# Tile offsets of 512 bytes, a feed-forward entered by 128 tokens first, and the order of matvec products

## Chip, core and metric

One core of a Trainium2 chip runs the whole program. The metric is the device time of one execution in microseconds, as the median of several runs. Numbers of the trace come from one further execution under the hardware profiler.

## What is computed

Two layers of a decoder trunk for 256 tokens of width 2048, all in float32. Every sub-layer adds `gate * f(RMSNorm(x) * (1 + scale) + shift)` to `x`, and the six vectors of a layer come from a conditioning vector `c` by one large matvec:

```python
cond = jax.nn.silu(c)
for l in range(DEPTH):
    mod = cond @ ada_w[l] + ada_b[l]
    sh1, sc1, g1, sh2, sc2, g2 = jnp.split(mod, N_MOD, axis=-1)
    h = modulate(rmsnorm(x, norm_mix_g[l]), sh1, sc1)
    y = mixer_ab(h, ...) if l % 2 == 0 else mixer_c(h, ...)
    x = x + g1[:, None, :] * y
    h = modulate(rmsnorm(x, norm_ffn_g[l]), sh2, sc2)
    x = x + g2[:, None, :] * swiglu(h, ffn_w1[l], ffn_w3[l], ffn_w2[l])
return rmsnorm(x, final_g)
```

`swiglu` is `(silu(h @ w1) * (h @ w3)) @ w2` with 5632 hidden columns. `mixer_ab` (layer 0) has an input projection to 4096 columns, a causal convolution over 31 tokens on one half, a gated mixing within chunks of 128 tokens on the other, and an output projection; `mixer_c` (layer 1) pools over 2 to 16 tokens.

## The kernel before

**Products.** A float32 product is made of three products of a shorter type: both operands are split into a high part (`hi` of a weight, `ah`, `mh` or `hh` of an activation) and the rest (`lo`; `al`, `ml`, `hl`), and hi x high, hi x rest and lo x high are added up in one PSUM bank (lines 255, 256 and 261). The tokens are the stationary side: 128 columns of an activation tile are loaded as weights, and 512 columns of a weight tile stream by. Weights are loaded by SyncE as `raw` tiles of 512 KB (two blocks of 128 rows by 512 columns, 12 buffers), and `split` (L206, L207) makes `hi` on ScalarE and `lo` on VectorE, with 4 buffers each. A `unit` does 512 rows of one weight for both halves of the tokens (b = 0 and 1): 24 products. A `block` splits two units ahead and runs all their products for b = 0, then all for b = 1, and calls hooks on the way. Activations of the mixers and of the first feed-forward product stand in `ah`/`al` (`mh`/`ml` share these places), the hidden ones, which the second product `w2` reads, in `hh`/`hl`, in a pool that is opened after all the others.

**Where tiles lie.** Pools lie one behind the other in each partition, and each tile is rounded up to 32 bytes. As built, the activation tiles begin at byte 36,384 of a partition, `raw` at 69,152, `hi` at 118,304 and `lo` at 134,688, and all their sizes are multiples of 512: each of them begins 32 bytes past a multiple of 512. The work pool's tiles begin at 171,552. The pool of the hidden tiles `hh`/`hl` begins at 195,936, which is 352 past a multiple of 512, and all of its tiles have this offset.

**Matvecs.** The `ada_w` products run in the background, in steps between units (`tick`, with a rate of steps per unit in RATES). Some vectors are made on TensorE: `mod` (L354) and `mod_cols` (L420) load two raw tiles a step and issue four matmuls of 32 rows, j = 0, 1 from the tile loaded first and j = 2, 3 from the one loaded last, into four strips of one bank. Others are summed up on VectorE (`weighed`, L390 and L392), with a column sum (`ps_col`, L448) at the end. `shift[0]` and `shift[1]` are the two halves of the vector that shifts the first feed-forward's input.

**The seam into the first feed-forward.** The mixer's output projection ends in `tail`: a block whose b = 0 products come first, so that the residual (L707, L708), the squares (L507) and the norm (`rstd`: L514, L516, and `r` on GpSimd, L518) of the first 128 tokens start while b = 1 runs. `ffn` then calls `e.prep` for the other quarters and for b = 1: `xr` (here on ScalarE, since `lean` is set, L527), four transposes (L532), a copy `xT` (L570). `started` closes the generators of the first quarter's scale and shift, makes `h`, `ah` and `al` (L552 or L554, L541, L542) for both halves, and runs three units for each quarter q of the 2048 input columns; the third one's banks are `mt`. Between units it advances the generators of the next quarters. Instructions of one engine run in the order in which a scheduler put them at build time, with semaphores between engines.

Of the kernel before, what the change touches and what calls it, by code (L numbers as in the profile page):

```python
# [8 lines left out]
F32 = mybir.dt.float32  # L9
F32R = mybir.dt.float32r  # L10
AF = mybir.ActivationFunctionType
ALU = mybir.AluOpType
PSUM = bass.MemoryType.PSUM
ENG = mybir.EngineType
# [3 lines left out]
P = 128  # L18
# [9 lines left out]
PADC = 16  # L28
EPS = 1e-6
RAW, HL = 12, 4  # L30
RATES = 1.28, 0.71, 0.5, 1.0, 1.0
PE2 = False
PE3 = True
FILL = 5
# [6 lines left out]
class Trunk:  # L41
# [6 lines left out]
    def __init__(self, ctx, tc, ins, out):  # L48
        self.ctx, self.tc, self.nc = ctx, tc, tc.nc
        self.i, self.out = ins, out  # L50
        self.bg = []
        self.credit = 0.0
        self.late = []
        self.fill = []
        self.lean = False

        def pool(name, bufs, **kw):
            return ctx.enter_context(tc.tile_pool(name=name, bufs=bufs, **kw))

        self.cpool = pool("const", 1)  # L60
        self.xpool = pool("resid", 1)
        self.apool = pool("act", 1)
        self.rawp = pool("raw", RAW)
        self.hip = pool("whi", HL)
        self.lop = pool("wlo", HL)
        self.accp = pool("acc", 1)
        self.gp = pool("gate", 2)
        self.wk = pool("work", 2)
        self.mmp = pool("mmp", 4, space=PSUM)
        self.tpp = pool("tpp", 2, space=PSUM)  # L70
        self.adap = pool("adap", 1, space=PSUM)
        self.msp = pool("msp", 1, space=PSUM)


    def consts(self):
        nc, c = self.nc, self.cpool
        i = self.i
        warm = c.tile([P, 1], F32, name="warm")
        nc.vector.memset(warm, 0.0)
        nc.scalar.activation(warm, warm, AF.Silu)  # L80
        self.ident = c.tile([P, P], F32, name="ident")
        make_identity(nc, self.ident)
        self.identr = c.tile([P, P], F32R, name="identr")
        nc.vector.tensor_copy(self.identr, self.ident)
        self.ones = c.tile([P, P], F32, name="ones")
        nc.vector.memset(self.ones, 1.0)
        self.mhalf = c.tile([P, 1], F32, name="mhalf")
        nc.gpsimd.memset(self.mhalf, -0.5)
        self.pick = c.tile([P, 1], F32, name="pick")
        nc.gpsimd.memset(self.pick, 0.0)  # L90
        for j in range(4):
            nc.gpsimd.memset(self.pick[32 * j : 32 * j + 1, :], 1.0)
# [251 lines left out]
    def mod(self, l, v, on_pe, then):  # L344


        nc = self.nc
        w = self.i["ada_w"][l]
        if on_pe:
            ps = self.adap.tile([P, 512], F32, name="ps_ada", tag="ada")  # L350
            for k in range(KT):
                raws = [self.load_wide(w, k * P, v * D + DH * h)[0] for h in range(2)]
                for j in range(4):
                    nc.tensor.matmul(  # L354
                        ps[32 * j : 32 * j + 32, :], self.cond[:, k : k + 1].to_broadcast([P, 32]),
                        raws[j // 2][:, j % 2, :], start=k == 0, stop=k == KT - 1, skip_group_check=True,
                    )
                if k < KT - 1:
                    yield
        else:  # L360
            ps = None
            for hh in range(2):
                acc = self.accp.tile([P, DH], F32, name="acc", tag="acc")
                for _ in self.weighed(acc, l, v * D + DH * hh):
                    yield
                if ps is None:
                    ps = self.adap.tile([P, 512], F32, name="ps_ada", tag="ada")
                for j in range(2):
                    o = 32 * (2 * hh + j)
                    nc.tensor.matmul(  # L370
                        ps[o : o + 32, :], self.ones[:, :32], acc[:, 512 * j : 512 * j + 512],
                        start=True, stop=True, skip_group_check=True,
                    )
                if hh == 0:
                    yield
        rows = self.wk.tile([P, 512], F32, name="rows", tag="rows", bufs=1)
        nc.vector.tensor_tensor(
            rows, ps, self.load_rows(self.i["ada_b"][l, v * D : (v + 1) * D]), op=ALU.add
        )
        then(rows)  # L380
        yield
# [25 lines left out]
    def mod_cols(self, l, v, q, on_pe, dst, gname=None, staged=False):  # L407
# [6 lines left out]
            acc = self.accp.tile([P, 512], F32, name="accq", tag="acc")  # L414
        for u in range(4):
            raws = [self.load(self.i["ada_w"][l], 512 * u + 256 * h, v * D + 512 * q) for h in range(2)]
            for j in range(4):
                k = 4 * u + j
                if on_pe:
                    nc.tensor.matmul(  # L420
# [100 lines left out]
    def transposed(self, b, q, r):  # L521
# [1 line left out]
        nc = self.nc  # L523
        xr = self.wk.tile([P, 512], F32, name="xr", tag="t", bufs=3)
        src = self.x[b][:, 512 * q : 512 * q + 512]
        if self.lean:
            nc.scalar.activation(xr, src, AF.Copy, scale=r)  # L527
        else:
            nc.vector.tensor_scalar(xr, src, r, None, op0=ALU.mult)
        ps = self.tpp.tile([P, 4, P], F32, name="tp", tag="tp")  # L530
        for a in range(4):
            nc.tensor.transpose(ps[:, a, :], xr[:, P * a : P * a + P], self.ident)  # L532
# [115 lines left out]
    def started(self, e, w_cols, rate):  # L648

        self.rate = 0.0
        ps = [self.banks(), self.banks()]
        ps.append([self.tpp.tile([P, 512], F32, name=f"mt{b}", tag="tp") for b in range(NB)])
        for g in e.parts[0]:
            self.close(g)
        for q in range(4):
            e.act[q] = [self.scaled(e.act[q][b], q, b, e.gs, e.sh) for b in range(NB)]
            nxt = e.parts[q + 1] if q < 3 else ()
            more = e.parts[2][1:] if q == 0 else ()  # L660
            for u, (w, col0) in enumerate(w_cols):
                self.unit(
                    w, 512 * q, col0, e.act[q], ps[u], q == 0, q == 3, lambda: self.between(nxt, 2 * u, more)
                )
                self.between(nxt, 2 * u + 1, more)
        self.rate = rate
        return ps

# [41 lines left out]
            self.sumsq(b, q)  # L710


    def mixer_ab(self, e, nxt):
        nc, i = self.nc, self.i
        with ExitStack() as s:
            p = s.enter_context(self.tc.tile_pool(name="ab", bufs=1))
# [57 lines left out]
                for _ in extra:  # L774
                    pass
            self.rate = RATES[0]
            self.lean = True
            act = e.act

            co = p.tile([P, HT, T], F32, name="co", tag="co")  # L780
# [138 lines left out]
            def out_half(half):  # L919
                for n in range(4):  # L920
# [5 lines left out]
                        self.residual(ps[b], self.g1, n, b, half == 0)  # L926

                    if half == 0 and n == 3:
                        self.tail(cells, resid, nxt)
                    else:  # L930
                        self.chain(cells)
# [72 lines left out]
    def ffn(self, p, l, e, nxt, gen_g2, rest):  # L1004
# [4 lines left out]
        held = {}  # L1009
        act = e.act  # L1010
        if e.parts:
            for q in range(1, 4):
                e.prep(0, q)
            for q in range(4):
                e.prep(1, q)
            ps = self.started(e, [(w1, 0), (w3, 0), (w1, 512)], RATES[1])
            self.lean = False
            held = {(1, 0): ps[0], (3, 0): ps[1], (1, 1): ps[2]}
        else:
            ps = self.begun(e, [(w1, 0), (w3, 0), (w1, 512)], rest)  # L1020
# [74 lines left out]
    def run(self):  # L1095
# [16 lines left out]
        self.gen_g1 = self.add(self.bcast(0, G1, True, self.g1))  # L1112
        scale = [self.mod_cols(0, SC2, q, True, ffn0.gs, "ffn_g") for q in range(4)]
        shift = [self.mod_full(0, SH2, ffn0.sh, None, (hh,)) for hh in range(2)]
        self.add(*scale, *shift)
        ffn0.parts = [(scale[0], shift[0]), scale[1:2], (scale[2], shift[1]), scale[3:]]
        self.mixer_ab(mix0, ffn0)

        self.g2 = self.gate()
        g2 = self.add(self.bcast(0, G2, False, self.g2))  # L1120
# [77 lines left out]
```

## Time and profile before

| | |
|---|---|
| median of 3 runs | 2008.23 us (2002.36 to 2008.52) |
| the profiled execution | 2001.65 us, of it a span of 1999.9 us |
| mean granted TensorE clock | 0.984 |
| TensorE matmuls busy | 1950.2 us, 8896 records |
| VectorE / ScalarE busy | 1408.9 / 849.8 us |
| HBM | 536.68 MB read, 269 GB/s over the span |

Times in views are microseconds from the span's start unless marked ns. A row of a group reads: line, engine, operation, out<-in, shapes, count, then busy time and the mean ns of one, then idle time of the engine before it and what ended it. A matmul's own duration overlaps the next one's, so the pace is read from starts or from counts in a window. In rows of the timeline the first two numbers are start and duration. In the chain of work the second is what the piece adds to it.

### The profile page before, as it was taken

The page shows a single profiled execution, that of the slowest core. Times are in us where ns is not written, and L with a number is a line of the kernel's source. Part 1 is how long each engine was busy: PE and PEld are TensorE (multiplying, and loading weights), DVE is VectorE, ACT ScalarE, POOL GpSimd, SP SyncE. Part 2 cuts the span into 40 slices and gives each one's busy share as a digit, 9 for nine tenths or more (in the row PEclk, how much of TensorE's full clock was granted, in tenths as well). Part 3 has the DMA queues.
Part 4 walks back from the last instruction along what each step waited for, and adds up shares of the span by engine and source line. Part 5 has one row for each costly group of instructions (what it writes and reads, how often), then busy time and mean ns, then how long its engine had stood idle before and what let it go on. Part 6 is the DMA issues. An engine that isn't in the chain of part 4 may idle for free.

```text
span 1999.9 us, 24247 instructions
## 1 busy us (share of the span) xinstructions
PE 1950.2 (98%) x8896; PEld 1539.9 (77%) x8896; DVE 1408.9 (70%) x1650; ACT 849.8 (42%) x1047; POOL 33.9 (2%) x92
## 2 busy tenths in 40 slices
PE   6899999989999999999999999999999999999998
PEld 3566667768887888887878877888788888888886
DVE  2678999796878878777887788877455445554455
ACT  3244343465444334433344346544434444334443
POOL 0000000000000000000210000000000000000000
PEclk7899999989999999999999999999999999999999
DMA  9998988798989899888988887988556665566551
GB/s 350 366 358 281 339 273 277 277 343 278 322 299 327 314 311 347 313 295 304 327 325 297 281 289 264 332 280 309 194 189 190 190 190 191 178 196 192 189 184 48
DMA packets 246248, 540.39 MB, mean 270 GB/s; under 512 B 16521, under 2 KB 17849, under 8 KB 245744
## 3 DMA queue, kind: packets, MB, share of 16 engines
q1 hardware_dynamic: 245840, 537.79, 77.9%
q8 instruction: 69, 1.13, 0.2%
q10 hardware_dynamic: 288, 1.05, 0.1%
q14 instruction: 51, 0.42, 0.1%
HBM read 536.68 MB, written 2.10 MB: 269 GB/s over the span
## 4 chain that ended last, share of the span: by engine, by line
PE 93%; DMA 3%; DVE 2%; ACT 1%; issue 0%; SPq 0%; POOL 0%; POOLq 0%; DVEq 0%; ACTq 0%
PE mm L255 28%; PE mm L256 27%; PE mm L261 27%; PE ps_ada L420 1%; DMA raw<-in_ab_w_in_dram 1%; PE ps_col L448 1%; PE mt L255 1%; PE tp L699 1%; PE mt L256 1%; PE mt L261 1%; PE ps_ada L354 1%; PE tp L532 1%; DMA x<-in_x_dram 1%; DVE accq L427 1%; DMA raw<-in_ada_w_dram 1%; PE tp L965 1%
## 5 line engine op out<-in xcount | busy, mean ns | idle before, releaser
L206 ACT CAST hi<-raw 128x1024 fp32r<-128x1024 f32 x632 | 663.8, 1052 | 1010.9 <-PE mm L256 902.8
L207 DVE TENSOR_TENSOR lo<-raw,hi 128x1024 fp32r<-128x1024 f32 x632 | 771.0, 1224 | 426.0 <-ACT hi L206 419.2
L255 PE MATMUL mm<-hi,ah 128*128 128x512 f32 x1568 | 618.7, 395 | 4.7 <-ACT hi L206 3.7
L256 PE MATMUL mm<-hi,al 128*128 128x512 f32 x1568 | 613.5, 391 | 0.0
L261 PE MATMUL mm<-lo,ah 128*128 128x512 f32 x1568 | 422.1, 390 | 0.0
L255 PEld LDWEIGHTS mm<-hi,ah 128*128 128x128 f32 x1568 | 295.6, 189 | 89.3 <-ACT hi L206 16.0
L261 PEld LDWEIGHTS mm<-lo,ah 128*128 128x128 f32 x1568 | 295.0, 188 | 61.6
L256 PEld LDWEIGHTS mm<-hi,al 128*128 128x128 f32 x1568 | 296.0, 189 | 60.2
L255 PE MATMUL mm<-hi,hh 128*128 128x512 f32 x704 | 278.9, 396 | 0.0
L256 PE MATMUL mm<-hi,hl 128*128 128x512 f32 x704 | 278.1, 395 | 0.0
L392 DVE SCALAR_TENSOR_TENSOR acc<-raw,cond,acc 128x1024 f32<-128x1024 f32 x210 | 269.1, 1281 | 7.0 <-DMA raw<-in_ada_w_dram 5.1
L261 PE MATMUL mm<-lo,hh 128*128 128x512 f32 x704 | 194.7, 395 | 0.0
L255 PEld LDWEIGHTS mm<-hi,hh 128*128 128x128 f32 x704 | 132.0, 187 | 33.9 <-ACT hi L206 1.7
L261 PEld LDWEIGHTS mm<-lo,hh 128*128 128x128 f32 x704 | 132.0, 187 | 32.2
L256 PEld LDWEIGHTS mm<-hi,hl 128*128 128x128 f32 x704 | 132.1, 188 | 31.8
L803 DVE SCALAR_TENSOR_TENSOR co<-aT,cw,co 128x256 f32<-128x256 f32 x240 | 100.1, 484 | 0.0
L420 PE MATMUL ps_ada<-raw,cond 128*32 128x512 f32 x352 | 60.9, 659 | 6.4 <-DMA raw<-in_ada_w_dram 5.7
L255 PE MATMUL mm<-hi,mh 128*128 128x512 f32 x160 | 65.1, 408 | 1.6 <-ACT mh L541 1.6
L256 PE MATMUL mm<-hi,ml 128*128 128x512 f32 x160 | 64.6, 406 | 0.3 <-DVE ml L542 0.3
L707 DVE TENSOR_TENSOR gy<-mm,gate 128x512 f32<-128x512 f32 x72 | 47.0, 686 | 23.9 <-PE mm L261 23.6
L427 DVE SCALAR_TENSOR_TENSOR accq<-raw,cond,accq 128x512 f32<-128x512 f32 x75 | 56.3, 751 | 9.7 <-DMA raw<-in_ada_w_dram 7.8
L255 PE MATMUL mt<-hi,ah 128*128 128x512 f32 x96 | 40.7, 424 | 7.2 <-ACT hi L206 7.2
(170 smaller groups left out, 993.7 us busy)
## 6 DMA issues: line engine op xcount, KB each, us to landing
raw<-in_ffn_w_dram SPq DMA_DIRECT2D x528, 512.0 KB, 4.8
raw<-in_ada_w_dram SPq DMA_DIRECT2D x384, 512.0 KB, 5.6
raw<-in_ab_w_in_dram SPq DMA_DIRECT2D x64, 512.0 KB, 7.9
raw<-in_ab_w_out_dram SPq DMA_DIRECT2D x32, 512.0 KB, 6.6
raw<-in_pool_w_dram SPq DMA_DIRECT2D x8, 512.0 KB
x<-in_x_dram SPq DMA_DIRECT2D x2, 1024.0 KB
gate<-in_final_g_dram SPq DMA_DIRECT2D x1, 1024.0 KB
out_dram<-x SPq DMA_DIRECT2D x2, 512.0 KB, 3.8
```

What stands on the lines that cost most here:

```text
L206: nc.scalar.copy(hi, raw)
L207: nc.vector.tensor_tensor(lo, raw, hi.bitcast(F32), op=ALU.subtract)
L255: nc.tensor.matmul(ps[b], act[b][0][:, kk, :], hi[:, k, :], start=first and kk == 0, stop=False)
L256: nc.tensor.matmul(ps[b], act[b][1][:, kk, :], hi[:, k, :], start=False, stop=False)
L261: self.nc.tensor.matmul(ps[b], act[b][0][:, kk, :], lo[:, k, :], start=False, stop=last and kk == 3)
L354: nc.tensor.matmul(ps[32 * j : 32 * j + 32, :], self.cond[:, k : k + 1].to_broadcast([P, 32]), raws[j // 2][:, j % 2, :], start=k == 0, st ...
L392: nc.vector.scalar_tensor_tensor(acc, raw, self.cond[:, k : k + 1], acc, op0=ALU.mult, op1=ALU.add)
L420: nc.tensor.matmul(acc[32 * j : 32 * j + 32, :], self.cond[:, k : k + 1].to_broadcast([P, 32]), raws[j // 2][:, j % 2, :], start=u == 0, s ...
L427: nc.vector.scalar_tensor_tensor(acc, raws[j // 2][:, j % 2, :], self.cond[:, k : k + 1], acc, op0=ALU.mult, op1=ALU.add)
L448: nc.tensor.matmul(ps[:, a : a + 1], src[:, P * a : P * a + P], one, start=u == 0, stop=u == len(parts) - 1,)
L707: nc.vector.tensor_tensor(t, ps, g[:, 512 * q : 512 * q + 512], op=ALU.mult)
L803: nc.vector.scalar_tensor_tensor(co[:, k, :], src, cw[:, k, j : j + 1], co[:, k, :], op0=ALU.mult, op1=ALU.add,)
```

## The change

Four things change.

Offsets: two constants of one column each become one tile, and a tile of 192 bytes that nothing uses stands at the head of the work pool. As built, the activation tiles begin at 36,352, `raw` at 69,120, `hi` at 118,272, `lo` at 134,656 and the hidden tiles at 196,096, all of which are multiples of 512. The work pool's other tiles begin 192 past one.

Matvecs on TensorE: the four products of a step go in the order 2, 3, 0, 1. The background's rate in the first mixer is 1.31 in place of 1.28.

Seam: the scale and `shift[0]` generators are finished ahead of the mixer's `tail`; `shift[1]` is added behind the mixer. `started` makes the first quarter's tile for b = 0 alone, runs the first two units as a `block` (24 products for b = 0, then 24 for b = 1) and calls the other `prep`s and the scaling for b = 1 from its hooks. `xr` is always made on VectorE, and `lean` holds inside `started` alone.

```diff
-RATES = 1.28, 0.71, 0.5, 1.0, 1.0
+RATES = 1.31, 0.71, 0.5, 1.0, 1.0
...
         self.wk = pool("work", 2)
+        self.wk.tile([P, 48], F32, name="gap", tag="gap", bufs=1)
...
-        self.mhalf = c.tile([P, 1], F32, name="mhalf")
+        two = c.tile([P, 2], F32, name="two")
+        self.mhalf, self.pick = two[:, :1], two[:, 1:]
         nc.gpsimd.memset(self.mhalf, -0.5)
-        self.pick = c.tile([P, 1], F32, name="pick")
...
                 raws = [self.load_wide(w, k * P, v * D + DH * h)[0] for h in range(2)]
-                for j in range(4):
+                for j in (2, 3, 0, 1):
...
             raws = [self.load(self.i["ada_w"][l], 512 * u + 256 * h, v * D + 512 * q) for h in range(2)]
-            for j in range(4):
+            for j in (2, 3, 0, 1) if on_pe else range(4):
...
-        if self.lean:
-            nc.scalar.activation(xr, src, AF.Copy, scale=r)
-        else:
-            nc.vector.tensor_scalar(xr, src, r, None, op0=ALU.mult)
+        nc.vector.tensor_scalar(xr, src, r, None, op0=ALU.mult)
...
         ps = [self.banks(), self.banks()]
+        act = e.act[0]
+
+        def scale(b):
+            act[b] = self.scaled(act[b], 0, b, e.gs, e.sh)
+
+        self.soon(scale, 0)
+        todo = [(e.prep, 1, 0), (e.prep, 0, 1), (e.prep, 1, 1), (scale, 1), (e.prep, 0, 2), (e.prep, 1, 2), (e.prep, 0, 3)]
+        slots = [(0, 1), (0, 2), (0, 3), (1, 0), (1, 1), (1, 2), (1, 3)]
+        self.block(
+            [(w, 0, col0, act, ps[u], True, False) for u, (w, col0) in enumerate(w_cols[:2])],
+            {at: [lambda c=c: self.soon(*c)] for at, c in zip(slots, todo)},
+        )
+        e.prep(1, 3)
         ps.append([self.tpp.tile([P, 512], F32, name=f"mt{b}", tag="tp") for b in range(NB)])
-        for g in e.parts[0]:
-            self.close(g)
+        self.lean = True
         for q in range(4):
-            e.act[q] = [self.scaled(e.act[q][b], q, b, e.gs, e.sh) for b in range(NB)]
+            if q > 0:
+                e.act[q] = [self.scaled(e.act[q][b], q, b, e.gs, e.sh) for b in range(NB)]
             nxt = e.parts[q + 1] if q < 3 else ()
             more = e.parts[2][1:] if q == 0 else ()
+            if q == 0:
+                last = [n for n in self.nc.cur_bb.bb.instructions if n.engine == ENG.DVE][-1]
+                with self.tc.issue_after(last):
+                    for slot in range(2):
+                        self.between(nxt, slot, more)
             for u, (w, col0) in enumerate(w_cols):
+                if q == 0 and u < 2:
+                    continue
                 self.unit(
-                    w, 512 * q, col0, e.act[q], ps[u], q == 0, q == 3, lambda: self.between(nxt, 2 * u, more)
+                    w, 512 * q, col0, e.act[q], ps[u], q == 0, q == 3,
+                    lambda: (self.between(nxt, 2 * u), self.between((), 0, more)),
                 )
-                self.between(nxt, 2 * u + 1, more)
+                self.between(nxt, 2 * u + 1)
+                for _ in range(2):
+                    self.between((), 0, more)
+        self.lean = False
...
                     if half == 0 and n == 3:
+                        self.finish(scale)
                         self.tail(cells, resid, nxt)
...
-            for q in range(1, 4):
-                e.prep(0, q)
-            for q in range(4):
-                e.prep(1, q)
             ps = self.started(e, [(w1, 0), (w3, 0), (w1, 512)], RATES[1])
-            self.lean = False
...
-        self.add(*scale, *shift)
+        self.add(*scale, shift[0])
+        last_shift = shift[1]
...
-        self.mixer_ab(mix0, ffn0)
+        self.mixer_ab(mix0, ffn0, [*scale, shift[0]])
+        self.add(last_shift)
```

In the order of the built program, TensorE at the seam before: `ps_col` is the column sum of `shift[0]`, `tp` the transposes, `ah_3506`/`al_3507` the first quarter's tile for b = 0.

```order
L448 MATMUL ps_col<-ones,acc 128x1 x8
L532 MATMUL tp<-ident,xr 128x128 x24
L255 MATMUL mm_3495<-hi,ah_3506 128x512
L532 MATMUL tp<-ident,xr 128x128 x4
L256 MATMUL mm_3495<-hi,al_3507 128x512
L532 MATMUL tp<-ident,xr 128x128 x4
```

And now, where `ah_3434`/`al_3435` are that tile:

```order
L262 MATMUL mm_3315<-lo,mh_2917 128x512 x2
L530 MATMUL tp<-ident,xr 128x128 x12
L256 MATMUL mm_3425<-hi,ah_3434 128x512
L257 MATMUL mm_3425<-hi,al_3435 128x512
L530 MATMUL tp<-ident,xr 128x128 x4
L256 MATMUL mm_3425<-hi,ah_3434 128x512
L257 MATMUL mm_3425<-hi,al_3435 128x512
L530 MATMUL tp<-ident,xr 128x128 x4
```

The column sum has gone ahead, into the mixer's tail; 12 transposes in place of 24 stand before the first product (of b = 0 and, among them, of b = 1), and the rest between products.

VectorE at the same place before: `s` and `m` lead to the norm, `gy`/`x` are the residual of the mixer's last columns, `sh` is the shift from the column sum.

```order
L707 TENSOR_TENSOR gy<-mm_3292,gate 128x512
L392 SCALAR_TENSOR_TENSOR acc<-raw,cond,acc 128x1024
L708 TENSOR_TENSOR x_114<-x_114,gy 128x512
L392 SCALAR_TENSOR_TENSOR acc<-raw,cond,acc 128x1024
L207 TENSOR_TENSOR lo<-raw,hi 128x1024
L514 TENSOR_REDUCE s<-ss 128x1
L454 TENSOR_TENSOR sh_119<-ps_col,adab 128x8
L516 TENSOR_SCALAR m<-s 128x1
L390 TENSOR_SCALAR acc<-raw,cond 128x1024
L707 TENSOR_TENSOR gy<-mm_3293,gate 128x512
L392 SCALAR_TENSOR_TENSOR acc<-raw,cond,acc 128x1024
L708 TENSOR_TENSOR x_115<-x_115,gy 128x512
```

And now:

```order
L208 TENSOR_TENSOR lo<-raw,hi 128x1024 x2
L515 TENSOR_REDUCE s<-ss 128x1
L517 TENSOR_SCALAR m<-s 128x1
L527 TENSOR_SCALAR xr<-x_114,r 128x512
L730 TENSOR_TENSOR gy<-mm_3315,gate 128x512
L731 TENSOR_TENSOR x_115<-x_115,gy 128x512
L552 TENSOR_SCALAR h_3429<-xT_3393,gs_118,sh_119 128x128 x2
L515 TENSOR_REDUCE s<-ss 128x1
L517 TENSOR_SCALAR m<-s 128x1
L527 TENSOR_SCALAR xr<-x_115,r 128x512
L527 TENSOR_SCALAR xr<-x_114,r 128x512
L540 TENSOR_TENSOR al_3435<-h_3429,ah_3434 128x512
```

The sums of `shift[1]` (L390, L392; L391, L393 now) no longer stand among these; the first of them comes behind the last `xr`, eight rows further down. Two splits stand before the first half's `s`, and the second half's norm and `xr` before the first half's `al`.

TensorE at the column sum of `shift[1]` before, within the second quarter's second unit (`ah_3656`):

```order
L261 MATMUL mm_3497<-lo,ah_3656 128x512 x2
L261 MATMUL mm_3498<-lo,ah_3665 128x512 x2
L448 MATMUL ps_col<-ones,acc 128x1 x8
L255 MATMUL mm_3497<-hi,ah_3656 128x512
L256 MATMUL mm_3497<-hi,al_3657 128x512
```

And now, where `ah_3810` is the third quarter's first tile, which needs that shift:

```order
L262 MATMUL mt_3582<-lo,ah_3656 128x512 x2
L262 MATMUL mt_3583<-lo,ah_3665 128x512 x2
L449 MATMUL ps_col<-ones,acc 128x1 x8
L256 MATMUL mm_3425<-hi,ah_3810 128x512
L257 MATMUL mm_3425<-hi,al_3811 128x512
```

The sum has moved behind the last product of the second quarter, right before the first of the third.

More of the change, by code (lines that the diff above doesn't have):

```diff
@@ L710, in residual, with mixer_ab @@
             self.sumsq(b, q)
-    def mixer_ab(self, e, nxt):
+    def mixer_ab(self, e, nxt, scale):
         nc, i = self.nc, self.i
@@ L776, in mixer_ab @@
             self.rate = RATES[0]
-            self.lean = True
             act = e.act
```

## The prediction

> **What bounds the kernel now.** I read the page first (busy time, the chain that ended last), then busy time in windows, then single instructions in order of time at the places that the change touches.
>
> ```profile
> span 1999.9 us, 24247 instructions
> PE 1950.2 (98%) x8896; PEld 1539.9 (77%) x8896; DVE 1408.9 (70%) x1650; ACT 849.8 (42%) x1047; POOL 33.9 (2%) x92
> PE 93%; DMA 3%; DVE 2%; ACT 1%; issue 0%; SPq 0%; POOL 0%; POOLq 0%; DVEq 0%; ACTq 0%
> ```
>
> TensorE is busy 98% of the span and makes up 93% of the chain. So a microsecond counts only if TensorE gets it back: as idle time, or as a shorter step from one matmul to the next. The second looks closed until two stages are laid side by side, one of the last feed-forward's second product (weight loads from `hh`, `hl`) and one of its first (from `ah`, `al`):
>
> ```profile
> core 0: us, PE busy (x) PEld busy (x) DVE busy (x) ACT busy (x) POOL busy (x), PEclk, DMA share, GB/s
> 1725.00:1775.00 50.00, 50.00 (x216) 40.10 (x215) 27.60 (x27) 18.58 (x18) 0.00 (x0) 1.00 0.58 185
> 1625.00:1675.00 50.00, 50.00 (x226) 41.48 (x226) 24.45 (x22) 21.12 (x23) 0.00 (x0) 1.00 0.60 190
> ```
>
> ```profile
> L699 PE MATMUL tp<-ident,hm 128*128 128x128 f32 x8 | 1.0, 272 | 0.0
> ```
>
> Both are full, at the full granted clock, with the other engines half idle and the same DMA rate. In the second window 8 of the 226 are transposes of 1.0 us together (row above). So a product takes 50.0/216 = 231.5 ns in the first and 49.0/218 = 224.8 ns in the second, both a little low in the same way, since a matmul cut by an edge is counted: 6.7 ns apart. The starts say the same; here are the first and last row of a short run from each:
>
> ```profile
> 1739.70 0.39 PE L256 MATMUL mm<-hi,hl 128*128 128x512 f32 x1
> ...
> 1742.96 0.39 PE L256 MATMUL mm<-hi,hl 128*128 128x512 f32 x1
> ```
>
> ```profile
> 1640.01 0.39 PE L255 MATMUL mm<-hi,ah 128*128 128x512 f32 x1
> ...
> 1642.95 0.39 PE L256 MATMUL mm<-hi,al 128*128 128x512 f32 x1
> ```
>
> The first run has 14 steps in 3.26 us, 233 ns each; the second 13 in 2.94 us, 226 ns. Shape, type, moving tiles (`hi`, `lo`), banks and loop are the same. What differs is the tile that the weights are loaded from, and its place: `ah`, `al` begin 32 bytes past a multiple of 512, like `hi` and `lo`; `hh`, `hl` begin 352 past one. Nothing shows that the offset is the cause, but no other difference is left that I can find.
>
> **The change, part by part.** *Offsets.* `hh` and `hl` come to the same offset as `hi`, `lo`, `ah`, `al`: all 0. Their products, and the others, by the page:
>
> ```profile
> L255 PE MATMUL mm<-hi,hh 128*128 128x512 f32 x704 | 278.9, 396 | 0.0
> L256 PE MATMUL mm<-hi,hl 128*128 128x512 f32 x704 | 278.1, 395 | 0.0
> L261 PE MATMUL mm<-lo,hh 128*128 128x512 f32 x704 | 194.7, 395 | 0.0
> L255 PE MATMUL mm<-hi,ah 128*128 128x512 f32 x1568 | 618.7, 395 | 4.7 <-ACT hi L206 3.7
> L255 PE MATMUL mm<-hi,mh 128*128 128x512 f32 x160 | 65.1, 408 | 1.6 <-ACT mh L541 1.6
> L255 PE MATMUL mt<-hi,ah 128*128 128x512 f32 x96 | 40.7, 424 | 7.2 <-ACT hi L206 7.2
> ```
>
> 3 x 704 = 2112 products lose 6.7 ns each: 14.1 us. TensorE is the only full engine in these stages, so all of it comes off the end. The other 3 x (1568 + 160 + 96) = 5472 products already have equal offsets on both sides and only move with them by 32 bytes; I take nothing for them. Their bounds: a gain down to the shortest step for as many columns, which is that of the norm's sums (each of the ten streams 256 columns of plain fp32 twice),
>
> ```profile
> 347.26 2.16 PE ps_ln L813 x10
> ```
>
> 216 ns, so 5472 x 10.7 = 59 us on top of 2112 x 6.7 + 2112 x 10.7 = 37 us; and a loss up to the 233 ns of `hh`, 5472 x 6.7 = 37 us. The 226 ns are the nearest row, since the two offsets are equal there as they will be. [...]
>
> The DMAs' targets move too. They matter where loads set the pace, the first 150 us:
>
> ```profile
> 25.00:50.00 25.00, 21.03 (x89) 11.54 (x90) 9.90 (x20) 7.89 (x14) 0.00 (x0) 0.64 1.04 380
> ```
>
> No row has a load to another offset. Bounds: 0, or the matmuls' 3% of those 150 us, 4 us; I take 0. [...]
>
> *Seam into the first feed-forward.* Before, TensorE's own rows there are:
>
> ```profile
> 423.49 1.84 PE L448 MATMUL ps_col<-ones,acc 128*128 128x1 f32 x16
> 427.46 1.27 PE L532 MATMUL tp<-ident,xr 128*128 128x128 f32 x8 [2.14 <-ACT xr L527]
> 437.14 0.79 PE L255 MATMUL mm<-hi,ah 128*128 128x512 f32 x1
> 442.94 0.73 PE L255 MATMUL mm<-hi,ah 128*128 128x512 f32 x2 [1.00 <-ACT ah L541]
> 464.84 1.84 PE L448 MATMUL ps_col<-ones,acc 128*128 128x1 f32 x16
> 474.84 0.39 PE L255 MATMUL mm<-hi,ah 128*128 128x512 f32 x1
> ```
>
> ```profile
> PE tp L532 <- ACT xr L527: 6.6, 3, 3.8
> ```
>
> From the mixer's last product (423.49) to the first product of the third quarter (474.84) it takes 51.4 us: 144 products of 0.2267 (32.6), two column sums (3.7), waits of 6.6 + 1.0, and 7.5 in 32 transposes, some of it at half clock. What the first product needs afterwards, for the second half of the tokens, whose transposes stand in front of it in TensorE's order:
>
> ```profile
> 426.16 0.69 DVE L707 TENSOR_TENSOR gy<-mm,gate 128x512 f32<-128x512 f32 x1
> 431.10 0.16 DVE L514 TENSOR_REDUCE s<-ss 128x1 f32<-128x4 f32 x1
> 421.47 0.62 ACT L507 ACTIVATE junk<-x 128x512 bf16<-128x512 f32 x1
> L518 POOL TENSOR_TENSOR r<-m,mhalf x10: 547/552/1583, 15.0 to 1993.2; 128x1 f32<-128x1 f32 x10
> L529 DVE TENSOR_SCALAR xr<-x,r x16: 475/484/489, 15.6 to 1253.8; 128x512 f32<-128x512 f32 x16
> L207 DVE TENSOR_TENSOR lo<-raw,hi 128x1024 fp32r<-128x1024 f32 x632 | 771.0, 1224 | 426.0 <-ACT hi L206 419.2
> ```
>
> Residual 2 x 0.69, squares 0.8 with the read of the sum, two small steps 0.3, `r` 0.55, two `xr` 0.97, `al` 0.69: 4.7 us. On VectorE stand before it two splits (2.4) and the first half's `xr` (0.5); with about 0.1 for each hand-over the first product starts some 8.5 us after the mixer's last, where it took 437.14 - 423.49 = 13.7. The gain of about 5 us has two debits. The column sum of `shift[0]` is not gone, it stands in the mixer's tail now (1.8). And that of `shift[1]` no longer stands inside the second quarter's products but behind all of them, so that what follows it is uncovered. Before, from its landing to `al`:
>
> ```profile
> 466.71 0.17 DVE L454 TENSOR_TENSOR sh<-ps_col,adab 128x8 f32<-128x8 f32 x1 [2.99 <-PE ps_col L448]
> 469.50 0.69 DVE L542 TENSOR_TENSOR al<-h,ah 128x512 fp32r<-128x512 f32 x1 [1.48 <-ACT ah L541]
> ```
>
> That is a new wait of 2.8 us. Behind the waiting TensorE all products of the third quarter queue, and VectorE's splits for them, as their buffers come free. Afterwards, then: 8.5 + 32.6 + 20 transposes of 0.16 (3.2) + about 1 of half clock + 1.8 + 2.8 = 49.9, with the 1.8 moved ahead 51.7, against 51.4. I count 0. Ends: -7.6, all of the old waits gone and no new one; +4, if the sums for `shift[1]` are late. They begin only after the last `xr`, about 12 us in, and are 16 of 1.28 us among 12 splits of 1.22,
>
> ```profile
> L392 DVE SCALAR_TENSOR_TENSOR acc<-raw,cond,acc 128x1024 f32<-128x1024 f32 x210 | 269.1, 1281 | 7.0 <-DMA raw<-in_ada_w_dram 5.1
> ```
>
> so VectorE is through at about 12 + 35 = 47 us or a little later, and TensorE is there at 46. That the block runs 128 tokens alone at first adds and removes no product; it lets 24 of them go before the tiles of the other 128 are there.
>
> *Matvec order.* Four products of a step (each two records in the trace) run side by side and cost as much as one of them:
>
> ```profile
> 164.10 0.97 PE ps_ada L354 x2
> 165.66 0.99 PE ps_ada L354 x6
> 172.36 0.99 PE ps_ada L354 x8
> 185.68 1.85 PE ps_ada L354 x16
> ```
>
> A step torn apart (1 + 3) costs 0.97 more; two steps in a row save 0.13. By the order there are 8 torn steps before and 7 after, 12 rows of two steps before and 9 after: -0.97 + 0.4 = -0.6 us. Both halves must have landed before the step can end, either way, so the DMA waits stay. The rate of 1.31 moves the same background sums a little earlier; it removes none, and TensorE covers them: 0. `xr` on VectorE is counted in the seam.
>
> Sum: the profiled execution took 2001.65 us (1.75 around the span); 2001.65 - 14.1 + 0 - 0.6 = 1987.0. The median of the three runs, 2008.23, is 6.6 above that execution, which is nearer to the lowest, 2002.36. The changed kernel's median may stand at either level, 1987 or 1993; I name 1988.
>
> **The rivals.** *Every product gets faster* (0 is better than 32, not only equal on both sides). For: the 226 ns are 10 above the norm's sums. Against: those stream another type, and the offsets of `ah` and `hi` are equal already. At 216 ns throughout 59 + 37 = 96 us go: 1906; half of the way, 1953. [...] Chance 0.20.
>
> *The offset is not it*: the region where `hh` lies is slower, or something else of that stage. Then the 14.1 are not there and seam and matvec remain: 2001, from 1993 to 2006 with the seam's ends and a little noise. For: the two stages differ in more than one number of an address. Against: the equal windows above. Chance 0.13.
>
> *Zero is a bad offset*: weight load and moving tile read at once, and from 0 they get in each other's way as `hh` and `hi` do now. All 5472 products take 233 ns, `hh` stays: 2001.65 + 36.7 - 0.6 = 2038. It decides from 2.6 ns more per product on, which is when 5472 of them eat up the 14.1. Against: equal offsets give the shorter step today. Chance 0.05.
>
> **How the numbers follow.** Forecast 0.62, rivals 0.20, 0.13 and 0.05. Less than 0.3%, 6 us, can't be told from no change. Faster: the forecast and the first rival, 0.82. Same: the second rival where the seam stays within 6 us, 0.11. Slower: the third, and the second with the seam late and the level of the median against it, 0.07. The range goes to 2001, which holds the forecast with all its ends (1979 to 1998) and most of the second rival, and down to 1940, which holds about half of the first.
>
> **What would show it.** Right: in windows inside the second products 222 matmuls in 50 us where 216 stood, with those of `ah` at 226 as before; the three `hh` groups with some 14 us less; at the seam no wait of 3.8 for `xr`, but one of about 3 us for `ah` behind a column sum, and the third quarter starting about 51 us after the mixer's end. Wrong: `hh` still at 216; `ah` at more or fewer than 226 in 50 us; or a seam that gains or loses over 5 us.

## The result, and the profile after

The changed kernel takes 1992.87 us (median of 4 runs, 1989.14 to 1994.4) against 2006.13 us of the kernel before beside it: a ratio of 0.9933, with a 95% interval of 0.991 to 0.9956, that is 13 us less. The profiled execution took 1989.14 us. From the page after:

```profile
span 1987.4 us, 24266 instructions
...
PE 1931.2 (97%) x8896; PEld 1537.2 (77%) x8896; DVE 1412.9 (71%) x1662; ACT 846.5 (43%) x1035; POOL 33.8 (2%) x92
...
L256 PE MATMUL mm<-hi,hh 128*128 128x512 f32 x704 | 275.3, 391 | 0.0
...
L257 PE MATMUL mm<-hi,hl 128*128 128x512 f32 x704 | 274.2, 389 | 0.0
...
L262 PE MATMUL mm<-lo,hh 128*128 128x512 f32 x704 | 190.3, 389 | 0.0
```

The records overlap (0.39 us each at a step of 0.23), so these sums of busy time fall by less (11.9 us over the three rows) than the steps do. The pace is read from the same two windows as before, second product and first product of the last feed-forward:

```profile
1725.00:1775.00 50.00, 50.00 (x222) 41.38 (x222) 27.52 (x27) 19.15 (x19) 0.00 (x0) 1.00 0.61 194
1625.00:1675.00 50.00, 50.00 (x227) 41.48 (x226) 24.45 (x22) 22.16 (x25) 0.00 (x0) 1.00 0.60 190
```

222 where 216 stood, and 227 where 226 stood: the products of `hh` and `hl` are shorter, those of `ah` are as they were. By all starts of these products, pauses left out, the mean step of `hh` went from 233.3 to 226.9 ns, that of `ah` stayed at 227.1. The six stretches of second products, each from its first to its last start, are 13.3 us shorter in sum.

The loads at the start are faster; the last column of the windows is GB/s, 380 and 388 before. Below it the 145th product of the first mixer, which began at 113.57 before:

```profile
25.00:50.00 25.00, 20.29 (x96) 12.28 (x97) 10.57 (x21) 9.83 (x15) 0.00 (x0) 0.80 1.05 407
...
75.00:100.00 25.00, 20.57 (x98) 12.43 (x91) 17.43 (x23) 4.67 (x5) 0.00 (x0) 0.91 1.05 408
```

```profile
110.23 0.50 PE L256 MATMUL mm<-hi,ah 128*128 128x512 f32 x1
```

So 3.3 us are won before the first mixer's products fill TensorE. They are gone at the seam. TensorE there, from the mixer's last products to the first product of the fourth quarter:

```profile
421.11 0.61 PE L262 MATMUL mm<-lo,mh 128*128 128x512 f32 x2
425.20 0.55 PE L530 MATMUL tp<-ident,xr 128*128 128x128 f32 x3 [3.48 <-DVE xr L527]
...
430.81 0.78 PE L256 MATMUL mm<-hi,ah 128*128 128x512 f32 x1
...
467.57 1.95 PE L449 MATMUL ps_col<-ones,acc 128*128 128x1 f32 x16 [0.57 <-DVE acc L393]
472.35 0.80 PE L256 MATMUL mm<-hi,ah 128*128 128x512 f32 x1 [2.83 <-ACT ah L539]
...
480.31 0.39 PE L256 MATMUL mm<-hi,ah 128*128 128x512 f32 x1
...
491.19 0.39 PE L256 MATMUL mm<-hi,ah 128*128 128x512 f32 x1
```

```profile
471.00:476.00 5.00, 3.65 (x8) 2.39 (x9) 1.39 (x2) 5.00 (x14) 0.00 (x0) 0.50 0.94 366
```

The same two ends before:

```profile
423.03 0.62 PE L261 MATMUL mm<-lo,mh 128*128 128x512 f32 x2
...
491.16 0.39 PE L255 MATMUL mm<-hi,ah 128*128 128x512 f32 x1
```

From the mixer's end to the fourth quarter it takes 491.19 - 421.11 = 70.1 us now and took 68.1. The column sum of `shift[0]`, 1.8 us, stood inside that stretch before and stands in front of it now, so the seam lost 3.8 us. The first product does come early (9.7 us behind the last pair instead of 437.14 - 423.03 = 14.1), although TensorE still waits for `xr` there, 6.8 us in two waits where it was 6.6 in three. But behind the column sum of `shift[1]` TensorE waits 2.83 us, and then the granted clock is 0.50: the first 24 products of the third quarter take 480.31 - 472.35 = 8.0 us, where 24 steps of 0.2267 are 5.4. The first ten of these steps take 0.42 us or more each, the other 14 take 0.23 or 0.24.

### The profile page after: what moved, and what is told of

It is laid out like the page before. It is cut to its first block, busy times and chain, and to the rows that moved or that the text cites. A ratio compares the mean times of both kernels' runs of the same rounds, so it can differ in the third digit from the quotient of the medians.

```text
span 1987.4 us, 24266 instructions
## 1 busy us (share of the span) xinstructions
PE 1931.2 (97%) x8896; PEld 1537.2 (77%) x8896; DVE 1412.9 (71%) x1662; ACT 846.5 (43%) x1035; POOL 33.8 (2%) x92
## 4 chain that ended last, share of the span: by engine, by line
PE 77%; DVE 1%; DMA 0%; ACT 0%; issue 0%; POOL 0%; POOLq 0%; DVEq 0%
PE mm L256 24%; PE mm L257 24%; PE mm L262 24%; PE tp L722 1%; PE mt L256 1%; PE mt L257 1%; PE mt L262 1%; PE ps_col L449 1%; PE tp L988 1%; PE tp L530 0%; PE ps_ada L371 0%; PE ps_ada L421 0%; DVE accq L428 0%; DMA raw<-in_pool_w_dram 0%; PE ps_bc L477 0%; PE ps_bc L478 0%
## 5 line engine op out<-in xcount | busy, mean ns | idle before, releaser
L393 DVE SCALAR_TENSOR_TENSOR acc<-raw,cond,acc 128x1024 f32<-128x1024 f32 x210 | 268.9, 1281 | 16.6 <-DMA raw<-in_ada_w_dram 15.0
L262 PE MATMUL mm<-lo,hh 128*128 128x512 f32 x704 | 190.3, 389 | 0.0
L421 PE MATMUL ps_ada<-raw,cond 128*32 128x512 f32 x352 | 55.8, 675 | 12.2 <-DMA raw<-in_ada_w_dram 11.4
L731 DVE TENSOR_TENSOR x<-x,gy 128x512 f32<-128x512 f32 x72 | 47.4, 688 | 0.2
```

Of the source, the lines that this page charges most:

```text
L262: self.nc.tensor.matmul(ps[b], act[b][0][:, kk, :], lo[:, k, :], start=False, stop=last and kk == 3)
L393: nc.vector.scalar_tensor_tensor(acc, raw, self.cond[:, k : k + 1], acc, op0=ALU.mult, op1=ALU.add)
L421: nc.tensor.matmul(acc[32 * j : 32 * j + 32, :], self.cond[:, k : k + 1].to_broadcast([P, 32]), raws[j // 2][:, j % 2, :], start=u == 0, s ...
L731: nc.vector.tensor_tensor(xs, xs, t, op=ALU.add)
```

## The experiments

Twelve runs, each beside the kernel before. A ratio below 1 is faster; microseconds are the ratio's distance from 1 times the median before, 2002.8 to 2004.6 here. Where two figures against the changed kernel are given, they go by its two ratios, 0.9933 above and 0.9944 of its second run.

**Equal, but not at a multiple of 512.** The kernel before, with

```diff
         self.wk = pool("work", 2)
+        self.wk.tile([P, 48], F32, name="gap", tag="gap", bufs=1)
```

> The kernel before with one edit, the unused tile of 192 bytes: hh and hl come to 32 past a multiple of 512, where hi, lo, ah, al and the DMAs' targets already are. Theory (equal offsets of weight and moving tile give the short step): 222 or more matmuls of the second products in 50 us where 216 stood, 226.7 ns a step, 13 to 14 us less than before, and the loads at the start stay at 380 to 388 GB/s. Rival (a multiple of 512 is what counts): 233 ns and 216 as before, 0 us. Rival (the place in the partition, not the offset): 0 us.

Measured: 0.9932 (0.9917 to 0.9948), 13.6 us less.

```profile
1725.00:1775.00 50.00, 50.00 (x223) 41.39 (x222) 27.67 (x27) 19.00 (x19) 0.00 (x0) 1.00 0.64 192
...
75.00:100.00 25.00, 19.70 (x94) 11.91 (x92) 16.46 (x23) 3.48 (x4) 0.00 (x0) 0.93 1.05 388
```

The second products have the short step with every tile 32 past a multiple of 512, and the loads are as before. At 32 equal offsets are enough; one unused tile of 192 bytes is worth as much as the whole change.

**Both offset edits.** The same, and the two constants in one tile.

> The kernel before with both offset edits, so that all tiles begin at multiples of 512, and nothing else. Theory: 13 us less from the steps of hh and hl, and about 3 us less in the first 125 us, since the loads go to 0 in place of 32 there (407 GB/s where 380 stood): 15 to 17 us less than before, which is more than the whole change gained, as the seam gives the 3 us back. Rival (the faster loads come from the matvec order, not from the targets): 380 GB/s as before, 13 us less, as in the run with the offsets equal at 32.

Measured: 0.9917 (0.9902 to 0.9932), 16.6 us less.

```profile
75.00:100.00 25.00, 20.22 (x95) 12.24 (x90) 17.38 (x23) 4.67 (x5) 0.00 (x0) 0.91 1.05 407
```

The faster loads come with the targets at 0 (407 GB/s here, 388 with them at 32 in the run above). The intervals of this run and the one before it overlap, so that the 3.0 us between them are not shown by the times alone. The traces show them: the 145th product begins at 112.97 to 114.49 us in the five profiled executions with `raw` at 32 or 64, and at 109.83 to 111.00 in the nine with `raw` at 0 or 256, 3.3 us apart in the mean. At the 193rd product, some 17 us later, the two groups are still 3.1 us apart in the mean, but single executions scatter by as much: the changed kernel has it at 127.68 us in one and at 130.83 in the other.

**The matvec order alone.**

```diff
-                for j in range(4):
+                for j in (2, 3, 0, 1):
...
-            for j in range(4):
+            for j in (2, 3, 0, 1) if on_pe else range(4):
```

> The kernel before with the matvec order 2, 3, 0, 1 alone. Theory: 0.6 us less by the torn steps, which can't be told from no change; loads at 380 to 388 GB/s in the first 100 us. Rival (the order lets raw buffers go sooner and speeds the start): 407 GB/s and 3 us less in the first 125 us.

Measured: 0.9985 (0.9974 to 0.9995), 3.0 us less.

```profile
75.00:100.00 25.00, 19.76 (x92) 11.98 (x92) 16.81 (x22) 4.51 (x5) 0.00 (x0) 0.86 1.05 389
```

More than the 0.6 expected and shown as a gain, but the loads are no faster, so the rival's reason is not there. The profiled execution (2004.93 us) is the longest of the 12 and shows no gain as a whole. In order of time it is 3.1 us behind the kernel before at 254 us and 2.0 behind at 267: a step that is torn before (two records at 262.16, six at 263.80) stands whole there (eight at 265.82), and 1.1 us are gained. It fell behind between 114 and 127 us, where TensorE waits 2.8 us for the tile `wcT` instead of 1.7, and the granted clock at 118 to 124 us is 0.75 instead of 1.00. Of the two profiles of the changed kernel one shows this too (2.8 and 0.74) and the other doesn't (1.7 and 1.00), so the order alone doesn't decide it. Where the rest of the 3 us comes from stays open.

**The seam alone**: the changed kernel without the offset edits and with the old matvec order; the rate of 1.31 stays.

> The changed kernel with the offsets and the matvec order undone, so the seam and the rate of 1.31 alone. Theory: 0 to 2 us more than before: the first product of the feed-forward 8.5 to 9.5 us behind the mixer's last instead of 13.7, then a wait of about 3 us for ah behind the column sum of the second shift, and 2 to 3 us of half clock after it, so that the fourth quarter begins no earlier against the mixer's end than before. Rival (the seam is worth its 5 us and something else lost it in the whole change): 4 to 5 us less than before.

Measured: 1.0033 (1.0022 to 1.0045), 6.6 us more. Its waits of TensorE there are those of the changed kernel, but for the last, which is 0.6 there:

```profile
PE tp L529 <- DVE xr L526: 6.8, 2, 3.5
PE mm L255 <- ACT ah L538: 2.8, 1, 2.8
PE ps_col L448 <- DVE acc L392: 1.0, 1, 1.0
```

The seam as changed is a loss, and a larger one than the theory's 0 to 2 us. From the mixer's end to the fourth quarter this trace takes 499.57 - 428.89 = 70.7 us, so with the 1.8 of the column sum it loses 4.4 there against the 68.1 of before. The three parts add up: -16.6 - 3.0 + 6.6 = -13.0, where the whole change measured -13.3.

**A ladder of distances.** The changed kernel with pads that put the four column groups of `hh`/`hl` at 0, 64, 128 and 256 past a multiple of 512:

```diff
             for ci, n in enumerate(grp):
+                if gi == 0 and ci > 0:
+                    p.tile([P, (0, 16, 16, 32)[ci]], F32, name=f"pad{ci}", tag=f"pad{ci}")
                 p1 = up(1, n)
```

> The changed kernel with pads between the hidden tiles, so that the four column groups of hh and hl begin at 0, 64, 128 and 256 past a multiple of 512, while hi and lo stay at 0. Theory (the two offsets must be equal modulo 512): 226.7 ns a step for the first quarter of the rows, 233 for the other three, 9 to 10 us more than the changed kernel. Rival (equal modulo 128 is enough): 233 at 64 alone, 3 us more. Rival (a gradual price of the distance): steps that grow from 0 to 256. Rival (multiples of 64 are all alike): 226.7 everywhere, which the 233 of before, with a distance of 320, speaks against.

Measured: 0.9969 (0.9956 to 0.9982), 5 to 7 us more than the changed kernel. Second products take the groups in turn, 24 products each. Here the first product of each of four groups, and of the next round:

```profile
1720.51 0.39 PE L256 MATMUL mm<-hi,hh 128*128 128x512 f32 x1
...
1725.95 0.40 PE L256 MATMUL mm<-hi,hh 128*128 128x512 f32 x1
...
1731.55 0.39 PE L256 MATMUL mm<-hi,hh 128*128 128x512 f32 x1
...
1737.12 0.39 PE L256 MATMUL mm<-hi,hh 128*128 128x512 f32 x1
...
1742.57 0.39 PE L256 MATMUL mm<-hi,hh 128*128 128x512 f32 x1
```

By 24: 226.7 ns at 0, 233.3 at 64, 232.1 at 128, 227.1 at 256. A distance of 256 is as good as none (227.1 against 226.7), so that it isn't 512 that has to be equal, and 128, at 232.1, isn't enough. The 320 of before took 233.3 too, as 64 does here.

**The weights moved instead.** The changed kernel with `raw` at 64 and `hi`, `lo`, `hh`, `hl` at 320, while `ah`, `al` stay at 0:

```diff
+        self.rawp.tile([P, 16], F32, name="gap1", tag="gap1", bufs=1)
         self.hip = pool("whi", HL)
+        self.hip.tile([P, 64], F32, name="gap2", tag="gap2", bufs=1)
```

> The changed kernel with raw at 64, hi, lo, hh and hl at 320 past a multiple of 512, while ah and al stay at 0. Theory (unequal offsets cost 6.7 ns, whichever tile is off): the second products stay at 222 matmuls in 50 us, and the first ones fall from 226 to 216 to 220; 5472 products by 6.7 ns are 36 us more than the changed kernel, slower than before. Rival (only some distances cost, and from hi at 320 to ah at 512 it is 192): nothing, or a part of it. Loads go to 64: 388 GB/s at 75 to 100 us if the targets want more than 64 bytes of alignment, 407 if 64 is enough.

Measured: 0.9998 (0.9988 to 1.0008): slower than the changed kernel by 11 to 13 us, not by 36. The first row is a window of second products; the two starts are 72 products of `ah` apart.

```profile
1725.00:1775.00 50.00, 50.00 (x222) 41.42 (x221) 28.34 (x31) 19.40 (x19) 0.00 (x0) 1.00 0.61 192
```

```profile
1821.81 0.39 PE L258 MATMUL mm<-hi,ah 128*128 128x512 f32 x1
...
1838.29 0.39 PE L258 MATMUL mm<-hi,ah 128*128 128x512 f32 x1
```

```profile
75.00:100.00 25.00, 17.46 (x93) 10.36 (x92) 17.62 (x24) 4.42 (x5) 0.00 (x0) 0.98 1.05 388
```

16.48 us by 72 is 228.9 ns: `ah` lost 2 ns, 11 us over 5472 products, and `hh` at 320 beside `hi` at 320 lost nothing. Seen from `hi`, `ah` lies 192 further modulo 256. And loads to 64 past a multiple of 512 ran at 388 GB/s, as those to 32 past did.

**The second shift in quarters.** The changed kernel, with the shift of the third and of the fourth quarter of the columns made apart, each with its own column sum within the quarter before:

```diff
-        shift = [self.mod_full(0, SH2, ffn0.sh, None, (hh,)) for hh in range(2)]
+        shift = [self.mod_full(0, SH2, ffn0.sh, None, (0,))]
+        shift += [self.mod_cols(0, SH2, q, False, ffn0.sh) for q in (2, 3)]
```

> The changed kernel with the second shift made as two quarters, each with its own column sum inside the quarter before the one that needs it, so that products follow each sum. Theory (the wait behind the column sum and the half clock after it cost the seam its gain): no wait of 2.8 us for ah, no window at half clock at the third quarter, 5 to 8 us less than the changed kernel: about 0.990 of before. Rival (VectorE is the bound there and the wait only moves): within 2 us of the changed kernel, 0.993.

Measured: 0.9926 (0.9912 to 0.994), as the changed kernel. The third quarter starts without a wait, and the wait is back at the fourth:

```profile
488.49 1.02 PE L449 MATMUL ps_col<-ones,accq 128*128 128x1 f32 x8
...
492.34 1.22 PE L256 MATMUL mm<-hi,ah 128*128 128x512 f32 x2 [2.49 <-ACT ah L539]
```

VectorE's rows say why:

```profile
460.62 1.23 DVE L208 TENSOR_TENSOR lo<-raw,hi 128x1024 fp32r<-128x1024 f32 x1 [1.23 <-ACT hi L207]
463.34 1.23 DVE L208 TENSOR_TENSOR lo<-raw,hi 128x1024 fp32r<-128x1024 f32 x1 [1.50 <-ACT hi L207]
466.66 0.16 DVE L455 TENSOR_TENSOR sh<-ps_col,adab 128x4 f32<-128x4 f32 x1 [2.10 <-PE ps_col L449]
466.75 0.48 DVE L426 TENSOR_SCALAR accq<-raw,cond 128x512 f32<-128x512 f32 x1
```

It idles for 4.8 us, 2.7 for `hi` and 2.1 for the column sum, while sums are left to do: the next quarter's first sum (L426) writes the one accumulator, which the column sum on TensorE has to read first. So VectorE isn't short of time there. That the buffer is what holds the sums up is read from the code; the run below that widens it moves the column sums as well.

**The change without its seam**: the kernel before with the offset edits and the matvec order.

> The kernel before with both offset edits and the matvec order, so the changed kernel without its seam and with the rate of 1.28. Theory (the seam as changed loses 6 us, as it did alone): 5 to 7 us less than the changed kernel, about 0.990 of before. Rival (the seam cost that much only at the old offsets): as the changed kernel, 0.993.

Measured: 0.991 (0.9896 to 0.9925), 18.0 us less than before. Leaving the seam out is better by 5 to 7 us; its interval overlaps that of the changed kernel's first measurement and lies just below that of the second (0.9929 to 0.9959).

**The odd distances.** The changed kernel with `raw`, `hi`, `lo` at 256 and the groups of `hh`/`hl` at 32, 96, 160 and 224 behind them, by the same kinds of pads:

```diff
+        self.rawp.tile([P, 64], F32, name="gap1", tag="gap1", bufs=1)
         self.hip = pool("whi", HL)
...
+                if gi == 0:
+                    p.tile([P, (8, 16, 16, 16)[ci]], F32, name=f"pad{ci}", tag=f"pad{ci}")
```

> The changed kernel with raw, hi and lo at 256 past a multiple of 512, ah and al at 0, and the four column groups of hh and hl at 32, 96, 160 and 224 behind hi and lo modulo 256. Theory (the step depends on the distance modulo 256, with 226.9 ns at 0, 233 at 64, 232 at 128 and 229 at 192, as the runs so far show): 226.9 for ah and al, as their distance is a whole 256, and between 229 and 234 for the groups, with the most at 96 and the least at 224; 6 to 9 us more than the changed kernel. Rival (only 0 and multiples of 512 are free for tiles in the first products): ah and al slower, 20 us more or worse. Loads go to 256: 407 GB/s if multiples of 256 are enough, 388 if it has to be 512.

Measured: 1.0005 (0.9994 to 1.0016), 12 to 14 us more than the changed kernel.

```profile
1729.04 0.39 PE L257 MATMUL mm<-hi,hh 128*128 128x512 f32 x1
...
1734.63 0.40 PE L257 MATMUL mm<-hi,hh 128*128 128x512 f32 x1
...
1740.25 0.39 PE L257 MATMUL mm<-hi,hh 128*128 128x512 f32 x1
...
1745.85 0.40 PE L257 MATMUL mm<-hi,hh 128*128 128x512 f32 x1
...
1751.45 0.39 PE L257 MATMUL mm<-hi,hh 128*128 128x512 f32 x1
```

```profile
1640.00:1690.00 50.00, 50.00 (x226) 41.50 (x225) 24.58 (x23) 21.92 (x24) 0.00 (x0) 1.00 0.63 191
75.00:100.00 25.00, 20.99 (x99) 13.40 (x92) 17.61 (x23) 4.67 (x5) 0.00 (x0) 0.84 1.05 408
```

By 24: 232.9, 234.2, 233.3 and 233.3 ns. The curve that I expected, falling off on both sides of 96, isn't there: 32 and 224 cost the full price, 2112 x 6.6 = 14 us in sum. `ah` at a distance of 256 keeps its 226 in 50 us, and loads to 256 ran at 408 GB/s, as those to 0 do in the changed kernel.

**The seam mended.** The changed kernel with the second shift in quarters that share one accumulator of 1024 columns, the column sums being placed behind the first unit of the second quarter and the second unit of the third:

```diff
+        elif wide is not None:
+            if not wide:
+                wide.append(self.accp.tile([P, DH], F32, name="acc", tag="acc"))
+            acc = wide[0][:, 512 * (q % 2) : 512 * (q % 2) + 512]
```

> The changed kernel with the second shift as two quarters in one accumulator of 1024 columns, so that VectorE needn't wait for the first column sum before it begins the second quarter's sums, and with the column sums behind the first unit of the second quarter and behind the second unit of the third. Theory (the single accumulator and the late place made the wait come back at the fourth quarter in the run with quarters): no wait over 0.5 us of TensorE in the second to fourth quarter and the fourth quarter's first product 6 to 7 us earlier behind the mixer's end than in the changed kernel; 0.990 of before or less. Rival (VectorE has too much to do there, splits included): the wait moves to the splits, 0.993.

Measured: 0.9896 (0.988 to 0.9912), 1983.79 us, 20.8 us less than before and the fastest of all.

```profile
420.71 0.61 PE L262 MATMUL mm<-lo,mh 128*128 128x512 f32 x2
...
455.57 0.94 PE L453 MATMUL ps_col<-ones,acc 128*128 128x1 f32 x8
...
473.75 0.94 PE L453 MATMUL ps_col<-ones,acc 128*128 128x1 f32 x8
...
484.68 0.39 PE L256 MATMUL mm<-hi,ah 128*128 128x512 f32 x1
```

Both column sums stand among products, with no wait of TensorE from 432 to 520 us and a granted clock of 1.00 in every 5 us from 450 to 480. The fourth quarter begins 484.68 - 420.71 = 64.0 us behind the mixer's last pair where it was 70.1: 6.1 us, as expected. The accumulator and the places of the sums changed together, so what each is worth isn't shown. Nor is it shown by the times that this seam beats the old one, since the interval overlaps that of the run without the seam; in the traces it takes 64.0 + 1.8 = 65.8 us where the old one takes 68.1.

**The changed kernel again**, on the chip of the last two.

> The changed kernel itself once more, on the chip of these runs, as their measure: 0.992 to 0.994 of before, the same column sum ahead of the third quarter with a wait of about 2.8 us for ah, and half a clock behind it.

Measured: 0.9944 (0.9929 to 0.9959), a little above the range expected; the wait for `ah` is 2.8 us again. Its interval doesn't meet that of the mended seam; 0.0048 are 9.6 us, of which the trace gives the seam 6.

**The last ladder**: groups at 192, 320, 448 and 480, `hi`, `lo` at 0.

```diff
+                    p.tile([P, (48, 32, 32, 8)[ci]], F32, name=f"pad{ci}", tag=f"pad{ci}")
```

> The changed kernel with the four column groups of hh and hl at 192, 320, 448 and 480 past a multiple of 512, hi and lo at 0. Theory (only the distance modulo 256 counts): at 192 and 448 the 229 ns that ah and al showed at that distance, at 320 the 233 that 64 showed, at 480 the 233 of 224. Rival (every distance that is no multiple of 256 costs the same 5 to 7 ns, and the 229 of ah and al came of something else, such as the place of hi and lo themselves at 320): 232 to 234 at all four. By the first 8 us more than the changed kernel, by the second 13.

Measured: 0.9977 (0.9964 to 0.999), 7 to 9 us more than the changed kernel.

```profile
1723.20 0.39 PE L256 MATMUL mm<-hi,hh 128*128 128x512 f32 x1
...
1728.69 0.40 PE L256 MATMUL mm<-hi,hh 128*128 128x512 f32 x1
...
1734.29 0.40 PE L256 MATMUL mm<-hi,hh 128*128 128x512 f32 x1
...
1739.80 0.40 PE L256 MATMUL mm<-hi,hh 128*128 128x512 f32 x1
...
1745.39 0.39 PE L256 MATMUL mm<-hi,hh 128*128 128x512 f32 x1
```

By 24: 228.8 ns at 192, 233.3 at 320, 229.6 at 448, 232.9 at 480; by all starts 230.1, 233.3, 230.2 and 233.4. 448 does as 192 (230.2 and 230.1) and 320 as 64 (233.3 and 233.4): in these pairs the distance counts modulo 256.

## Why the prediction held, and where not

*Offsets: 14.1 us predicted.* Right in size and cause: 13.3 us in the trace, 13.6 in the run that made the offsets equal and did nothing else. The rival that the offset is not the cause fell with that run and with the ladders, where the pace changes from one column group to the next, back and forth, as their offsets do. What the prediction left open is narrower than it thought: multiples of 512 are not needed, a distance of 0 or 256 is enough (226.7 and 227.1 ns in one run).

*The other 5472 products: 0.* Right. `ah` keeps 226 to 227 in 50 us whether all tiles are at 32, at 0, or `hi` at 256 and `ah` at 0. So the rival that every product gets faster and the one that zero is a bad offset both fell. The bound of 216 ns, an estimate from the norm's sums (ten records of 128x256 in 2.16 us, each taken as 512 columns), was not reached by these products at any offset: the shortest mean by all starts is 226.9.

*DMA targets: 0 taken, 4 as the bound.* Mis-sized: about 3.3 us by the traces. The 0 was my choice, as no row of before had a load to another offset. The runs show 406 to 408 GB/s at 75 to 100 us with `raw` at 0 and 256, and 388 or 389 at 32 and 64, a difference of 5%.

*Seam: 0, from -7.6 to +4.* This is the step that failed. Most of its pieces came out well: the first product came 9.7 us behind the start of the mixer's last pair, where 9.0 was expected (8.5 from a mark 0.46 behind it); the new wait was put at 2.8 us and was 2.83; VectorE was to be through with the sums at 47 us or later, just about when TensorE got there, and TensorE waited 0.57 us for them. The sum stopped at the third quarter's first product, though, and took the clock behind the wait for full. It was at half (0.50 at 471 to 476 us) for the first ten of the next 24 products, which cost 2.5 us. With it the seam comes to +3.8 in the trace, near the upper end; alone it measured +6.6, outside it, of which its trace gives the seam 4.4. About 1 us more lies earlier, in the mixer's wait for `mh` (2.64 us in the changed kernel and with the seam alone, 1.57 before), which the prediction didn't touch. The trace of the seam alone also has a lower granted clock at two places, 0.77 at 357 to 372 us and 0.83 at 1245 to 1255, where before and the changed kernel have 0.89 and 1.00. The run with the odd distances, which has the same seam, shows both as well, so they come in some executions only, and their share of the 6.6 isn't resolved. One sign of the prediction didn't come, either: it expected no wait of 3.8 us for `xr`, and TensorE still waited for `xr` twice, up to 3.48 us.

*Matvec: -0.6.* Too small: -3.0 alone, from -5.2 to -1.0. The trace shows 1.1 of it, at the torn step that became whole; the rest is open.

The sum was made against a profiled execution, 1987.0, and that of the changed kernel took 1989.14, with the median 3.7 above it. So it came out near partly by luck, because two errors of opposite sign stood beside a large term that was right: by the runs loads and matvec gave 5.4 us more than predicted (3.0 and 2.4), while the seam gave 4 to 7 less. In medians the forecast was 2008.23 to 1988, 20 us less, and 13 came: the prediction saw two levels, 1987 and 1993, and named the lower, while the median came at the upper.

## What to carry over

Compare the pace of the same instruction between two stages at a full engine and full clock; a difference of 3% that no other engine explains may be in the addresses, as with the 233.3 ns of `hh` and the 227.1 of `ah` here, and pads of some bytes test it at once. When a wait of some microseconds is set into a stream of matmuls, add the time at a lower clock behind it, and place the sum so that products cover both: in the 5 us in which such a wait of 2.5 to 2.8 us ended, the granted clock was 0.50 in the changed kernel, 0.55 with the seam alone and 0.66 with the shift in quarters. Before calling an engine too busy, look whether it idles for a buffer with work still to do.

## What the runs showed of the hardware

In these runs the step of a 128x512 product of this type went with the distance between where the weight tile and the moving tile begin in a partition, modulo 256 bytes. By the mean of all starts in second products: 226.9 ns at 0 (the same at 256), 233.1 at 32, 233.4 at 64, 234.1 at 96, 232.3 at 128, 233.4 at 160, 230.1 at 192 and 233.4 at 224. Of these only 0 is free, and 192 is cheaper than its neighbours, which two runs and both kinds of product show (230.1 ns for `hh`, 229.0 for `ah`). Why so was not tried, nor was any distance that is no multiple of 32.

Loads of rows of 2 KB ran at 406 to 408 GB/s in the window from 75 to 100 us into tiles at multiples of 256 bytes (0 and 256 past a multiple of 512) and at 388 to 389 into tiles 32 or 64 past one. No load to 128 was tried.
